# Two hybrid decoder layers on one core: attention by pairs of heads, one load for x and the first weights, rotated queries from SBUF, and three pieces of work put elsewhere in the order

## The chip, the cores and the metric

The kernel runs on 1 core of one Trainium2 chip. The metric is the device time of one execution in microseconds (us). Three runs of the kernel before gave 914.79, 917.12 and 917.61 us, so the median is 917.12 us. A separate profiled execution took 915.54 us; its trace spans 913.8 us from the first to the last instruction.

## The reference, cut to what matters

Two layers, one after the other, on x of 256 tokens by 2048 channels, all in float32. Each layer makes one input projection whose columns feed three mixers (a short convolution, multi-head latent attention, RWKV-7), concatenates their gated results, makes one output projection and normalizes.

```python
for l in range(DEPTH):                       # DEPTH = 2
    u = x @ w_in[l]
    (cb, cc, ch, cg, cq, ckv, kpe, mg, rcols, rg) = _split(u, IN_SIZES)
    y_conv = _short_conv_branch(cb, cc, ch, cg, conv_w[l])
    y_mla = _mla_branch(cq, ckv, kpe, mg, q_norm_g[l], w_uq[l], kv_norm_g[l], w_ukv[l], cos, sin)
    y_rwkv = _rwkv7_branch(rcols, rg, ...)
    mix = jnp.concatenate([y_conv, y_mla, y_rwkv], axis=-1)
    x = _layer_norm(DEEPNORM_ALPHA * x + mix @ w_out[l], ln_g[l], ln_b[l])
```

The attention branch has 8 heads. Queries come from `rms(cq) @ w_uq` (128 plain and 64 rotated channels a head), keys and values from `rms(ckv) @ w_ukv` (128 each), and one rotated key part is shared by all heads. Scores are causal; the result is multiplied by `silu(mg)`.

## The kernel before

**Matrix products.** TensorE reads float32 rounded to a shorter form (`F32R`). For accuracy each operand is split into a rounded part and the remainder, and three products are summed: hi·hi, hi·lo, lo·hi (`mm3`, or two instructions in `in_group` where the moving operand holds hi and lo side by side). The split of a tile is one ScalarE copy and one VectorE subtraction (`split_in`, line 205; `split_w` for weights). All VectorE and ScalarE instructions issued through the wrapper carry line 138 in the profile.

**Stages of a layer.** The input projection runs over column groups of 512 in the order k, a, r, v, cq, cc, ch, cb, cg, rg (`MAIN`), then `mla_kv` (`pkv`), `mla_q` (`pq`), then the groups mg0 and mg1, then the output projection `out_proj` (`po` with `hi_wo`) in four groups of 512 columns. Each weight tile is loaded by SyncE (line 394), split, and used by 24 or 16 matmuls. Products accumulate in two PSUM buffers (`acc`) and must be copied out before the second group after them can start.

**What is interleaved.** The mixers are Python generators. `tick()` advances each of them once per weight tile, so their instructions are issued between the projection's matmuls. A planner then puts every engine's instructions in order by a simulated timeline and by priority (`high_priority(n)` moves work n places ahead: `AHEAD` is 1500, `EVICT` is 4000). The result is a fixed order per engine; on the chip an engine waits at the head of its own order. `after(a, b)` and `gather(m, list)` only tell the planner that one instruction comes behind another; on two engines they make no wait on the chip.

**Buffers.** SBUF tiles come from pools by tag. The tag `s8` has 9 buffers of 8 KB per partition, which hold x (4 of them, until mg1 is done), the RWKV operands (`bk`, `ar`, two `gs`, `bkt`, `uvt`), then `mc` (the convolution's result, split), keys `kn`, values `vs`, queries `qn`, and the split attention results. A tile gets the buffer that comes free next in the order of allocation: before the change that is `mc`, `kn`, `vs`, `qn`. `c4` has 5 buffers, `s4` has 6.

**Start.** `load_x` (line 218) and line 394 issue for each step of `STEPS` one load of x and one of the first weight group k: 1, 1, 2, 2, ... chunks of 128 rows. `warm_up` runs `WARM` = 8 matmuls on zeros (`pzero`) first.

**Attention.** `mla_attend` (line 1054) makes one visit per head: `values(h-3)`, `turn(h-2)` (transposes of the probabilities, `ptr`), `scores(h)` (`sc`, softmax), `split_qk(h+1)`, then `yield`: 11 visits. `mla_q` copies `qn` out of PSUM on ScalarE and rotates `qp` with VectorE straight from PSUM (`rope`: a product with cosT, four quarter products with sinT, a sum).

**End of attention.** `gated` multiplies by the gate and leaves its instruction in `st["mark"]`; `mla_gate` splits the result into `ma0`, `ma1`. `out_proj` gets the mark as `begin` and puts behind it a table load with a reciprocal root (`rstd`) on ScalarE, the loads of the residual `xr` and of the norm rows `gb` (lines 1316 and 1319, issued by ScalarE) and the load of `gr` (issued by GpSimd).

**Norm.** `add` adds a finished block to the residual, takes its statistics and multiplies it by the norm weight. `root(1)` makes the last half's statistics into `rstd` and `cw`. `keep_warm` runs `KEEP` = 10 matmuls (`pz`) while that chain is on VectorE.

Of the kernel before, what the change touches and what calls it, by code (L numbers as in the profile page):

```python
# [31 lines left out]
WARM = 8  # L32
# [53 lines left out]
def lay_out(inp):  # L86
# [5 lines left out]
    o["xT"] = inp["x"][0].T.reshape(NKC, P, S).transpose(1, 0, 2)  # L92
# [19 lines left out]
def hybrid_layers(ctx: ExitStack, tc: tile.TileContext, x, positions, xT, w_in, w_out, w_uq, w_ukv, par, wa_in, gb_in,  # L112
# [123 lines left out]
    def warm_up():  # L236

        z = s8("zero", (P, 512))
        V.memset(z, 0.0)
        zr = s8("zeror", (P, 512), F32R)  # L240
        V.tensor_copy(zr, z)
        pz = pm.tile([P, 512], F32, tag="m", name="pzero")
        for i in range(WARM):
            T.matmul(pz, zr[:, 0:P], zr, start=True, stop=True)
# [17 lines left out]
    def rope_tables():  # L262
        ang = sm.tile([P, S], F32, tag="rt", name="ang")
        nn = sm.tile([P, S], F32, tag="rt", name="nn")
        V.tensor_copy(ang, posi)
# [3 lines left out]
        V.tensor_scalar(nn, nn, magic, None, ALU.subtract)  # L269
        c1 = 6.28125  # L270
# [5 lines left out]
        V.tensor_scalar(ang, ang, lim, -lim, ALU.min, ALU.max)  # L276
        A.activation(sinT, ang, AF.Sin, scale=cs[:, K_SG:K_SG + 1])
# [98 lines left out]
    def load():  # L376
# [4 lines left out]
        raw = to = behind = None  # L381
# [10 lines left out]
        if raw is None:  # L392
            raw = wr.tile(shape, F32, tag="raw", name=f"w_{name}_{k0}")
# [346 lines left out]
    def rwkv_pairs(l, st):  # L740
# [29 lines left out]
        for c2 in range(2):  # L770
# [12 lines left out]
            yield  # L783
# [184 lines left out]
    def rope(dst, ps, name):  # L968

        tmp = sm.tile([P, S], F32, tag="rt", name=f"rt_{name}")  # L970
        V.tensor_tensor(dst, ps, cosT, ALU.mult)
        for q in range(4):
            o = slice(q * 32, q * 32 + 32)
            i = slice((q ^ 1) * 32, (q ^ 1) * 32 + 32)
            V.tensor_tensor(tmp[o, :], ps[i, :], sinT[o, :], ALU.mult)
        V.tensor_tensor(dst, dst, tmp, ALU.add)

    def mla_kv(l, st):
# [3 lines left out]
        vs = s8(f"vs{l}", (P, 2, HEADS, P), F32R)  # L982
        for h2 in range(4):
# [21 lines left out]
    def mla_q(l, st):  # L1005
# [3 lines left out]
        for g in range(4):  # L1009
# [40 lines left out]
    def split_keys(st, h):  # L1050
        t = st["qk"][h % 2]
        split_in(t[:, 0, P:384], t[:, 1, P:384], st["kn"][:, h, :])

    def mla_attend(l, st):
# [4 lines left out]
        def split_queries(h):  # L1059
            t = qk[h % 2]  # L1060
            split_in(t[:, 0, 0:P], t[:, 1, 0:P], qn[:, h, P:S])

        def split_qk(h):

            split_queries(h)
            split_keys(st, h)

        gates.clear()
        with tc.high_priority(AHEAD):
            for par in range(2):  # L1070
# [3 lines left out]
                V.tensor_tensor(of(o), qp[r, :, P:S], of(r).bitcast(F32), ALU.subtract)  # L1074
                split_queries(par)
# [3 lines left out]
        def scores(h):  # L1079
            ps = pm.tile([P, 384], F32, tag="m", name=f"sc{l}_{h}")  # L1080
            for q0, k1, o in ((0, 128, slice(0, 128)), (128, 256, slice(128, 384))):
                if q0 == 0:
                    T.matmul(ps[:, o], qn[:, h, 0:P], kn[:, h, 0:k1], start=True, stop=False)
# [17 lines left out]
            for i, o in both:  # L1101
                V.tensor_scalar(s[:, o], s[:, o], mx[:, 4 + i:5 + i], None, ALU.mult)
            live[h] = s

        def turn(h):
            s = live[h]
            pt = pm.tile([P, 3, P], F32, tag="m", name=f"ptr{l}_{h}")
            for i in range(3):
                T.transpose(pt[:, i, :], s[:, i * P:i * P + P], ident)
# [6 lines left out]
        def values(h):  # L1116
            hi, lo, p2 = live.pop(h)
            po = pm.tile([P, S], F32, tag="m", name=f"po{l}_{h}")
            T.matmul(po[:, P:S], vt[:, h, :], p2, start=True, stop=False, skip_group_check=True)
            for i, (v, p) in enumerate(((0, hi), (1, hi), (0, lo))):  # L1120
                T.matmul(po, vs[:, v, h, :], p, start=False, stop=i == 2, skip_group_check=True)
            A.copy(qn[:, h, :], po)

        for h in range(HEADS + 3):
            if h >= 3:
# [314 lines left out]
```

## Time and profile before

| What | before |
|---|---|
| runs, median | 917.12 us (914.79 to 917.61) |
| profiled execution, own time | 915.54 us |
| its span, first to last instruction | 913.8 us |
| TensorE matmul busy | 891.9 us, 98% |
| TensorE weight load busy | 784.9 us, 86% |
| VectorE busy | 689.0 us, 75% |
| ScalarE busy | 485.6 us, 53% |
| GpSimd busy | 23.0 us, 3% |
| loads from HBM | 158.61 MB, 179 GB/s with the writes |

The time minus the span is 1.74 us. PE is TensorE's matmuls, PEld its weight loads, DVE is VectorE, ACT ScalarE, POOL GpSimd, SP SyncE; "ACTq" and "SPq" are loads being issued. A row of the timeline reads: start, duration, engine, line, operation, tiles out<-in, shapes, count, and in brackets the idle time before it with what ended it. A row of the windows view reads: busy time and instruction count of each engine in that stretch, granted TensorE clock, DMA share, GB/s.

### The profile page before, as it was taken

How to read it: one execution, taken by the hardware profiler on the slowest of the kernel's cores; microseconds unless marked ns; L12 is line 12 of the kernel's file. 1: busy time of each engine (PE TensorE's matmuls, PEld its weight loads, DVE VectorE, ACT ScalarE, POOL GpSimd, SP SyncE). 2: the span in 40 equal slices, each digit the busy share in tenths (PEclk: the TensorE clock that was granted, in tenths of full speed). 3: DMA queues.
4: the chain of work that ended last, by engine and by line, in shares of the span. 5: the costliest groups of instructions: out<-in, count | busy, mean ns of one | idle time of the engine just before them, and what ended most of it. 6: DMA issues, size and time to landing. Idle time of an engine off the chain costs nothing.

```text
span 913.8 us, 15981 instructions
## 1 busy us (share of the span) xinstructions
PE 891.9 (98%) x6311; PEld 784.9 (86%) x6311; DVE 689.0 (75%) x1166; ACT 485.6 (53%) x753; POOL 23.0 (3%) x47
## 2 busy tenths in 40 slices
PE   8999999999999999999999999999999999999996
PEld 7888888888889898788898888888888898987895
DVE  6788979976669977466765889799766699863875
ACT  5677445454447566444246873554444566664430
POOL 1220000000000000000020000000000000000000
PEclk9999999999999999999999999999999999999998
DMA  8865664676444654596476556646754356546932
GB/s 317 251 181 164 206 176 127 193 200 171 142 126 147 185 162 141 169 342 205 160 230 185 141 182 197 172 131 202 191 179 135 105 179 186 159 124 202 338 124 92
DMA packets 67548, 164.97 MB, mean 181 GB/s; under 512 B 15431, under 2 KB 24695, under 8 KB 67463
## 3 DMA queue, kind: packets, MB, share of 16 engines
q1 hardware_dynamic: 59712, 150.36, 54.7%
q10 hardware_dynamic: 5072, 9.57, 3.3%
q0 software_dynamic: 2688, 4.03, 1.5%
q8 instruction: 49, 0.80, 0.4%
q14 instruction: 27, 0.21, 0.1%
HBM read 158.61 MB, written 5.32 MB: 179 GB/s over the span
## 4 chain that ended last, share of the span: by engine, by line
PE 92%; DVE 4%; ACT 1%; issue 1%; DMA 1%; ACTq 0%; SPq 0%; DVEq 0%
PE u_mg L437 6%; PE po L337 6%; PE po L338 6%; PE po L339 6%; PE u_cc L437 3%; PE u_cg L437 3%; PE u_v L437 3%; PE u_cq L437 3%; PE u_mg L439 3%; PE u_ch L437 3%; PE u_cb L437 3%; PE u_r L437 3%; PE u_rg L437 3%; PE u_a L437 3%; PE u_rg L439 2%; PE u_cg L439 2%
## 5 line engine op out<-in xcount | busy, mean ns | idle before, releaser
L138 DVE TENSOR_TENSOR lo_wo<-w_wo,hi_wo 128x1024 fp32r<-128x1024 f32 x57 | 69.2, 1224 | 52.7 <-ACT hi_wo L138 51.9
L138 ACT CAST hi_wo<-w_wo 128x1024 fp32r<-128x1024 f32 x57 | 59.4, 1051 | 66.0 <-PE po L339 43.6
L437 PE MATMUL u_mg<-x,hi_mg 128*128 128x512 f32 x256 | 89.6, 393 | 2.0 <-DVE rt_q L138 2.0
L439 PE MATMUL u_mg<-x,lo_mg 128*128 128x256 f32 x256 | 71.3, 278 | 0.0
L437 PEld LDWEIGHTS u_mg<-x,hi_mg 128*128 128x128 f32 x256 | 48.0, 187 | 12.6 <-ACT qk L138 1.8
L337 PE MATMUL po<-hi_wo,ma 128*128 128x512 f32 (+1 forms) x128 | 46.8, 365 | 2.1 <-ACT ma L138 2.1
L439 PEld LDWEIGHTS u_mg<-x,lo_mg 128*128 128x128 f32 x256 | 48.2, 188 | 0.0
L138 ACT CAST hi_mg<-w_mg 128x1024 fp32r<-128x1024 f32 x32 | 33.6, 1049 | 24.8 <-PE u_mg L437 12.3
L339 PE MATMUL po<-hi_wo,ma 128*128 128x512 f32 (+1 forms) x128 | 46.6, 364 | 0.0
L338 PE MATMUL po<-lo_wo,ma 128*128 128x512 f32 (+1 forms) x128 | 46.5, 363 | 0.0
L437 PE MATMUL u_a<-x,hi_a 128*128 128x512 f32 x128 | 45.5, 398 | 0.9 <-DVE kx L138 0.9
L437 PE MATMUL u_cg<-x,hi_cg 128*128 128x512 f32 x128 | 46.0, 400 | 0.0
L437 PE MATMUL u_cc<-x,hi_cc 128*128 128x512 f32 x128 | 45.8, 400 | 0.0
L437 PE MATMUL u_cq<-x,hi_cq 128*128 128x512 f32 x128 | 45.6, 396 | 0.0
L437 PE MATMUL u_v<-x,hi_v 128*128 128x512 f32 x128 | 45.3, 399 | 0.0
L437 PE MATMUL u_r<-x,hi_r 128*128 128x512 f32 x128 | 45.2, 394 | 0.0
L437 PE MATMUL u_rg<-x,hi_rg 128*128 128x512 f32 x128 | 45.1, 392 | 0.0
L138 DVE TENSOR_TENSOR lo_mg<-w_mg,hi_mg 128x1024 fp32r<-128x1024 f32 x32 | 38.9, 1222 | 8.2 <-ACT hi_mg L138 8.0
L437 PE MATMUL u_cb<-x,hi_cb 128*128 128x512 f32 x128 | 44.5, 394 | 0.0
L437 PE MATMUL u_ch<-x,hi_ch 128*128 128x512 f32 x128 | 44.5, 394 | 0.0
L339 PE MATMUL u_k<-x,lo_k 128*128 128x256 f32 x128 | 37.1, 290 | 1.0 <-DVE lo_k L138 1.0
L337 PE MATMUL u_k<-x,hi_k 128*128 128x256 f32 x128 | 36.9, 288 | 0.9 <-ACT hi_k L138 0.9
(414 smaller groups left out, 2803.4 us busy)
## 6 DMA issues: line engine op xcount, KB each, us to landing
w_wo<-in_w_out_dram SPq DMA_DIRECT2D x64, 512.0 KB, 4.3
w_mg<-in_w_in_dram SPq DMA_DIRECT2D x32, 512.0 KB, 4.4
w_a<-in_w_in_dram SPq DMA_DIRECT2D x16, 512.0 KB, 5.0
w_r<-in_w_in_dram SPq DMA_DIRECT2D x16, 512.0 KB, 3.9
w_v<-in_w_in_dram SPq DMA_DIRECT2D x16, 512.0 KB, 3.9
w_cq<-in_w_in_dram SPq DMA_DIRECT2D x16, 512.0 KB, 3.8
w_cc<-in_w_in_dram SPq DMA_DIRECT2D x16, 512.0 KB, 4.1
w_ch<-in_w_in_dram SPq DMA_DIRECT2D x16, 512.0 KB, 3.6
```

The costliest lines, as they stand in the source:

```text
L138: inst = call(*args, **kwargs)
L337: m = T.matmul(o, lh, rh, start=first, stop=False, skip_group_check=True)
L338: T.matmul(o, lh, rl, start=False, stop=False, skip_group_check=True)
L339: T.matmul(o, ll, rh, start=False, stop=last, skip_group_check=True)
L437: T.matmul(ps[:, b, :].rearrange("p (i t) -> p i t", i=2), hi[:, k, c], x2, start=k0 + k == 0, stop=False, skip_group_check=True)
L439: T.matmul(ps[:, b, 0:S], lo[:, k, c], x2[:, 0, :], start=False, stop=k0 + k == NKC - 1, skip_group_check=True)
```

## The change

1. The host lays x and layer 0's group k side by side, so `load_first` brings both in one load per step, into `s8` tiles. The tiles of zeros go to `c4`. `WARM` is 7.
2. `rope_tables` becomes a generator: it starts a tick after group k and gives way twice.
3. `rope` does the sine products first and the cosine product in place. `mla_q` copies `qp` out of PSUM on ScalarE and rotates it in SBUF, at priority `AHEAD`.
4. The convolution's split `mc` no longer waits for the end of the RWKV chain but for the allocation of `vs`, so the order in `s8` becomes `kn`, `vs`, `mc`, `qn`.
5. `mla_attend` visits two heads at a time (6 visits of two yields); `values` fills one PSUM tile for two heads and copies it out at once; first matmuls are planned behind the splits and softmaxes that they need; `p2` gets a pair-wide tile with two buffers instead of one.
6. `st["mark"]` is the ScalarE copy of the last `ma` split, so the residual, norm rows and table load of `out_proj` come behind it.
7. In `add`, the last block's product with the norm weight moves behind `cw`; `keep_warm` runs 3 narrow and 9 wide matmuls.

```diff
-WARM = 8
+WARM = 7
-    o["xT"] = inp["x"][0].T.reshape(NKC, P, S).transpose(1, 0, 2)
+    o["xT"] = np.concatenate([inp["x"][0].T.reshape(NKC, P, S), w[0, :, :, 0].reshape(NKC, P, 512)], 2).transpose(1, 0, 2)
...
-    def load_x(k0, n):
-        xt = c4(f"xt0_{k0}", (P, n, S))
-        in_turn(1, nc.sync.dma_start(xt, xT[:, k0:k0 + n, :]))
+    def load_first(k0, n):
+        t = s8(f"first{k0}", (P, n, S + 512))
+        in_turn(1, nc.sync.dma_start(t, xT[:, k0:k0 + n, :]))
         with tc.high_priority():
-            for j in range(0, n, 2):
-                m = min(2, n)
-                t, at = xs[(k0 + j) // 4], (k0 + j) % 4
-                split_in(t[:, 0, at:at + m, :], t[:, 1, at:at + m, :], xt[:, j:j + m, :])
+            to, at = xs[k0 // 4], k0 % 4
+            split_in(to[:, 0, at:at + n, :], to[:, 1, at:at + n, :], t[:, :, 0:S])
         if k0 == 14:
-            load_constants(xt[:, 0, :])
+            load_constants(t[:, 0, :])
+        return t[:, :, S:].rearrange("p k (i c) -> p i k c", i=2)
...
-        z = s8("zero", (P, 512))
+        z = c4("zero", (P, 512))
...
     def rope_tables():
+        yield from until("k0")
+        yield
...
         if name == "k0":
-            load_x(k0, nk)
-            raw = s4(f"w_first{k0}", shape) if k0 < 10 else None
+            raw = load_first(k0, nk)
+            ready[name, k0] = k0, split_w(raw, f"{name}_{k0}", None, None)
+            return
...
     def rope(dst, ps, name):
-        V.tensor_tensor(dst, ps, cosT, ALU.mult)
         for q in range(4):
...
+        V.tensor_tensor(dst, ps, cosT, ALU.mult)
         V.tensor_tensor(dst, dst, tmp, ALU.add)
...
         vs = s8(f"vs{l}", (P, 2, HEADS, P), F32R)
+        done.add(f"vs{l}")
...
                 A.copy(qn[:, 2 * g:2 * g + 2, :], pn)
-                rope(qp[:, g, :], pe_, f"q{l}_{g}")
+                A.copy(qp[:, g, :], pe_)
+            with tc.high_priority(AHEAD):
+                rope(qp[:, g, :], qp[:, g, :], f"q{l}_{g}")
...
-            p2 = sm.tile([P, P], F32, tag="p2", name=f"p2{l}_{h}", bufs=1)
+            if h % 2 == 0:
+                st["p2"] = sm.tile([P, 2, P], F32, tag="rs", name=f"p2{l}_{h}", bufs=2)
+            p2 = st["p2"][:, h % 2]
...
+        def values(i):
+            po = pm.tile([P, 2, S], F32, tag="m", name=f"po{l}_{i}")
+            for j in range(2):
+                h = 2 * i + j
+                hi, lo, p2 = live.pop(h)
+                m = T.matmul(po[:, j, P:S], vt[:, h, :], p2, start=j == 0, stop=False, skip_group_check=True)
+                if j == 0:
+                    gather(m, [st["soft"]] if i < HEADS // 2 - 1 else [])
+                for n, (v, p) in enumerate(((0, hi), (1, hi), (0, lo))):
+                    T.matmul(po[:, j, :], vs[:, v, h, :], p, start=False, stop=n == 2, skip_group_check=True)
+            A.copy(qn[:, 2 * i:2 * i + 2, :], po)
+        pairs = HEADS // 2
+        for i in range(pairs + 2):
+            if i >= 2:
+                values(i - 2)
+            for h in (2 * i, 2 * i + 1):
+                if 1 <= i <= pairs:
+                    turn(h - 2)
+            for h in (2 * i, 2 * i + 1):
+                if i < pairs:
+                    scores(h)
+                if h + 2 < HEADS:
+                    split_qk(h + 2)
...
-        st["mark"] = V.scalar_tensor_tensor(y, g, 0.5, y, ALU.mult, ALU.mult)
+        V.scalar_tensor_tensor(y, g, 0.5, y, ALU.mult, ALU.mult)
...
-            split_in(*hl2([m], i * 2), st["qn"][:, half * 4 + i * 2:half * 4 + i * 2 + 2, :])
+            st["mark"] = split_in(*hl2([m], i * 2), st["qn"][:, half * 4 + i * 2:half * 4 + i * 2 + 2, :])[0]
...
-        yield from until(f"chain{l}")
+        yield from until(f"vs{l}")
         m = t["mc"] = pair(f"mc{l}")
...
-            if (h, g) != (1, 0):
+            if (h, g) != (1, 0) and (h, at) != (1, 256):
                 V.tensor_tensor(z, z, gs[g][:, 0, at:at + n], ALU.mult)
...
+            if h:
+                z = zs[3][:, 1, 256:512]
+                after(V.tensor_tensor(z, z, gs[3][:, 0, 256:512], ALU.mult), v)
...
-            for _ in range(KEEP):
-                T.matmul(pz, ms[3][:, 0, 0, 0:P], ms[3][:, 0, 0:2, :], start=True, stop=True)
+            for i in range(KEEP + 2):
+                T.matmul(pz[:, 0:P] if i < 3 else pz, ms[3][:, 0, 0, 0:P],
+                         ms[3][:, 0, 0, 0:P] if i < 3 else ms[3][:, 0, 0:2, :], start=True, stop=True)
...
-                rope_tables()
+                run(rope_tables())
```

More of the change, by code (lines that the diff above doesn't have):

```diff
@@ L236, in warm_up @@
     def warm_up():
-        z = s8("zero", (P, 512))
+        z = c4("zero", (P, 512))
         V.memset(z, 0.0)
-        zr = s8("zeror", (P, 512), F32R)
+        zr = c4("zeror", (P, 512), F32R)
         V.tensor_copy(zr, z)
@@ L269, in rope_tables @@
         V.tensor_scalar(nn, nn, magic, None, ALU.subtract)
+        yield
         c1 = 6.28125
@@ L276, in rope_tables @@
         V.tensor_scalar(ang, ang, lim, -lim, ALU.min, ALU.max)
+        yield
         A.activation(sinT, ang, AF.Sin, scale=cs[:, K_SG:K_SG + 1])
@@ L380, in load @@
             return
-        raw = to = behind = None
+        to = behind = None
         src = src[:, :, k0:k0 + nk, :] if len(src.shape) == 4 else src[:, k0:k0 + nk, :]
@@ L391, in load @@
             to = t[:, 0], t[:, 1]
-        if raw is None:
-            raw = wr.tile(shape, F32, tag="raw", name=f"w_{name}_{k0}")
+        raw = wr.tile(shape, F32, tag="raw", name=f"w_{name}_{k0}")
         i = nc.sync.dma_start(raw, src)
@@ L782, in rwkv_pairs @@
             A.copy(qs[:, c2 * 2:c2 * 2 + 2], pq_)
-            yield
+        yield
         st["qs"] = qs
@@ L1051, in split_keys @@
         t = st["qk"][h % 2]
-        split_in(t[:, 0, P:384], t[:, 1, P:384], st["kn"][:, h, :])
+        st[f"split{h}"] = [split_in(t[:, 0, P:384], t[:, 1, P:384], st["kn"][:, h, :])[1]]
     def mla_attend(l, st):
@@ L1060, in split_queries @@
             t = qk[h % 2]
-            split_in(t[:, 0, 0:P], t[:, 1, 0:P], qn[:, h, P:S])
+            return split_in(t[:, 0, 0:P], t[:, 1, 0:P], qn[:, h, P:S])[1]
         def split_qk(h):
-            split_queries(h)
+            v = split_queries(h)
             split_keys(st, h)
+            st[f"split{h}"].append(v)
         gates.clear()
@@ L1073, in mla_attend @@
                 A.copy(of(r), qp[r, :, P:S])
-                V.tensor_tensor(of(o), qp[r, :, P:S], of(r).bitcast(F32), ALU.subtract)
-                split_queries(par)
+                v = V.tensor_tensor(of(o), qp[r, :, P:S], of(r).bitcast(F32), ALU.subtract)
+                st[f"split{par}"] += [v, split_queries(par)]
+        st["split0"] += st["split1"]
         live = {}
@@ L1082, in scores @@
                 if q0 == 0:
-                    T.matmul(ps[:, o], qn[:, h, 0:P], kn[:, h, 0:k1], start=True, stop=False)
+                    m = T.matmul(ps[:, o], qn[:, h, 0:P], kn[:, h, 0:k1], start=True, stop=False)
+                    gather(m, st[f"split{h}"])
                     T.matmul(ps[:, o], qp[:, h // 2, 0:P], kpe[:, h % 2 * P:h % 2 * P + P], start=False, stop=True)
@@ L1101, in scores @@
             for i, o in both:
-                V.tensor_scalar(s[:, o], s[:, o], mx[:, 4 + i:5 + i], None, ALU.mult)
+                v = V.tensor_scalar(s[:, o], s[:, o], mx[:, 4 + i:5 + i], None, ALU.mult)
             live[h] = s
+            st["soft"] = v
         def turn(h):
@@ L1113, in turn @@
+            p2 = st["p2"][:, h % 2]
             A.copy(p2, pt[:, 2])
             live[h] = hi, lo, p2
[L1116 to L1122, printed above, removed]
@@ L1124, in mla_attend @@
-        for h in range(HEADS + 3):
-            if h >= 3:
-                values(h - 3)
-            if 2 <= h < HEADS + 2:
-                turn(h - 2)
-            if h < HEADS:
-                scores(h)
-            if 2 <= h + 1 < HEADS:
-                split_qk(h + 1)
-            if h == 3:
+        def values(i):
[9 more added lines that the diff above has]
+            A.copy(qn[:, 2 * i:2 * i + 2, :], po)
@@ L1134, in mla_attend @@
+        pairs = HEADS // 2
[10 more added lines that the diff above has]
+                    split_qk(h + 2)
+            if i == 2:
                 done.add(f"heads{l}")
-            if h >= 4 and h % 2 == 0 and f"mg{(h - 4) // 4}{l}" in done:
-                gated(l, st, (h - 4) // 2)
+            if i >= 2 and f"mg{(i - 2) // 2}{l}" in done:
+                gated(l, st, i - 2)
+            yield
```

4 lines of the change are left out of this document (3 added, 1 removed).

## The prediction, made before the changed kernel ran

> **What bounds the kernel now.** I read the page first: the span, the busy line, the chain that ended last.
>
> ```profile
> span 913.8 us, 15981 instructions
> PE 92%; DVE 4%; ACT 1%; issue 1%; DMA 1%; ACTq 0%; SPq 0%; DVEq 0%
> L437 PE MATMUL u_mg<-x,hi_mg 128*128 128x512 f32 x256 | 89.6, 393 | 2.0 <-DVE rt_q L138 2.0
> ```
>
> TensorE sets the end: 92% of the chain is matmuls. The change takes no matmul out but one of eight on zeros at the start, and adds some filler in `keep_warm`. It can only win where TensorE stands still. So the second view is who TensorE waited for, in total, over the whole run (us, times, longest):
>
> ```profile
> PE pkv L337 <- ACT vt L138: 2.9, 2, 1.4
> PE po L337 <- ACT ma L138: 2.1, 2, 1.0
> ...
> PE cwt L1259 <- DVE cw L138: 1.4, 1, 1.4
> PE u_k L339 <- DVE lo_k L138: 1.0, 2, 0.8
> PE xt L1280 <- PE pz L1312: 0.9, 1, 0.9
> PE u_k L337 <- ACT hi_k L138: 0.9, 1, 0.9
> PE u_a L437 <- DVE kx L138: 0.9, 1, 0.9
> PE po L338 <- DVE lo_wo L138: 0.5, 2, 0.3
> ...
> PE pq L337 <- ACT qn L138: 0.4, 1, 0.4
> PE pq L337 <- ACT vt L138: 0.4, 1, 0.4
> ```
>
> With the 2.0 us of `rt_q` in the row above these are 13.4 us. That is nearly all that this change can reach: about 1.5% of the span, in ten places, each with another cause. The busy shares of VectorE and ScalarE say little here; in each place it is one late instruction that matters. I go through the places in the order of the change's parts.
>
> **Start: one load for x and w, seven matmuls on zeros.** The chain, then four windows, then two rows of single instructions:
>
> ```profile
> 3.78 5.88 DMA w_first<-in_w_in_dram
> 9.69 1.05 ACT hi_k L138
> ...
> 12.04 0.38 PE u_k L339
> ```
>
> ```profile
> 0.00:4.00 4.00, 1.97 (x5) 1.60 (x6) 1.46 (x4) 1.69 (x2) 1.45 (x6) 1.00 0.38 121
> 4.00:8.00 4.00, 4.00 (x19) 3.63 (x17) 1.32 (x3) 1.84 (x4) 0.00 (x0) 1.00 0.86 258
> 8.00:12.00 4.00, 2.19 (x15) 1.57 (x13) 2.28 (x4) 2.19 (x4) 0.00 (x0) 1.00 1.01 364
> 16.00:20.00 4.00, 4.00 (x36) 4.00 (x35) 3.61 (x5) 3.07 (x5) 0.00 (x0) 1.00 1.05 388
> ```
>
> ```profile
> 10.64 0.61 ACT L138 CAST x<-xt 128x512 fp32r<-128x512 f32 x1
> L244 PE MATMUL pzero<-zeror 128*128 128x512 f32 x8 | 3.8, 652 | 2.0 <-DVE zeror L138 2.0
> ```
>
> Steady matmuls begin at 12.04, when the weights of the third step are split; they landed at 9.69, and that load was the sixth to be issued, at 3.78. In the new kernel it is in the third load. The first three loads hold 4 x 128 rows x 768 numbers x 4 bytes = 1.57 MB. The old kernel had moved 0.48 MB by 4.0 (121 GB/s); the other 1.09 MB take 3.0 us at the 364 GB/s of the third window and 4.2 at the 258 of the second. So they land at 7.0 to 8.2, that is 1.5 to 2.7 earlier. Off that goes the cast of x (0.61), which arrives with the weights now and is ahead of them on ScalarE: 0.9 to 2.1. I take 1.6. If the merged load lands no sooner, x's cast makes it 0.6 worse; the bounds are -0.6 and 2.1. After these a step is 0.79 MB, 2.2 us at 364 GB/s, and its 24 matmuls take 2.7 (36 in 4.00 us, the fourth window), so an early start isn't lost again there. The matmul on zeros that goes is 3.8/8 = 0.47 us ahead of the first `u_k`; it is inside the 1.6, since the wait at 12.04 decides. The new tiles share `s8`: five are free, and later loads wait for a split, not the first three.
>
> At 652 ns a matmul on zeros is slower than the 393 of `u_mg` of the same shape. The Trainium skill (TensorE: Matmul & The Clock Gate, Part 1) says that the array starts at half rate and that a time of activity, not a count of matmuls, ends this. By that rule the `u_k` matmuls that move forward by 0.47 us run at half rate, and an estimate of the start's gain would be 1.4 in place of 1.6 us.
>
> **Tables of the rotation as a generator.** `u_a` waits 0.9 us for the last `kx`, which frees the accumulator. ScalarE is at this then:
>
> ```profile
> 39.63 1.28 ACT L138 ACT_TABLE_LOAD   x1
> ```
>
> That is the load for the sines, between the third and the fourth `kx`. Planned a few ticks later, it comes behind `kx`. I take 0.7 of 0 to 0.9. What is late next is the rotated key, which nothing on TensorE needs before attention.
>
> **Values' buffer.** ScalarE's and TensorE's timelines, layer 0:
>
> ```profile
> 266.64 0.57 ACT L138 COPY kn<-pkv 128x512 f32<-128x512 f32 x1
> 271.48 0.65 ACT L138 CAST vs<-pkv 128x256 fp32r<-128x256 f32 x2
> ```
>
> ```profile
> 271.24 0.69 PE L808 MATMUL py<-st,ar 64*64 64x64 f32 x32
> 273.37 0.39 PE L337 MATMUL pkv<-hkv,hi_ukv 128*128 128x256 f32 x1 [1.43 <-ACT vt L138]
> ```
>
> Keys leave PSUM at 266.64, values of the same group only at 271.48, when the RWKV chain's last products are running: `vs` holds the buffer that comes free last. The third `pkv` group then waits 1.43 us for the accumulator. In the new order `vs` takes the place in the line that `kn` had, `kn` that of `mc`, both free by 266.64, and `mc` is left with the late one. Then the copies come at once and the 2.9 us of both layers go, perhaps the 0.4 of `pq` behind it too. I take 2.9 of 1.4 to 3.3. `mc` costs this:
>
> ```profile
> L337 PE MATMUL po<-hi_wo,mc x16: 387/389/398, 354.9 to 381.3; 128*128 128x512 f32 x16
> L138 DVE TENSOR_TENSOR mc<-cy,mc x2: 687/690/692, 245.9 to 246.5; 128x512 fp32r<-128x512 f32 x2
> ```
>
> Its split is needed at 354.9 and has 80 us; but two times 0.69 us of VectorE per layer move from 246 to after 272, into the stretch that is full (next part). Price 0 to 2.8; I take 1.0.
>
> **Rotation from SBUF.** TensorE in layer 1, then VectorE, ScalarE and the window in layer 0:
>
> ```profile
> 752.49 0.47 PE L437 MATMUL u_mg<-x,hi_mg 128*128 128x512 f32 x1 [1.62 <-DVE rt_q L138]
> ```
>
> ```profile
> 298.95 1.72 DVE L138 TENSOR_TENSOR rt_q<-pq,sinT 32x256 f32<-32x256 f32 x4
> 295.19 0.58 ACT L138 COPY qn<-pq 128x512 f32<-128x512 f32 x1
> 296.00:300.00 4.00, 4.00 (x34) 4.00 (x35) 3.93 (x7) 1.83 (x4) 0.00 (x0) 1.00 0.50 140
> ```
>
> The accumulator is held by VectorE's rotation, and VectorE is busy 3.93 of 4.00 us. ScalarE, busy 1.83, takes the copy: half of the 128x512 that cost 0.58 us, so between 0.29 and 0.58. VectorE's own work doesn't shrink; its five products only leave the accumulator's way. Of 2.0 us I take 1.6 (0 to 2.0): one of the copies may stand behind a weight cast, as `qn` did for the 0.4 of the waits, and for that and the eight copies I put a cost of 0.4 (0 to 1.6).
>
> **End of attention, and heads by two.** ScalarE, TensorE, then VectorE's first use of the residual, layer 1:
>
> ```profile
> 835.54 1.28 ACT L138 ACT_TABLE_LOAD   x1
> 836.95 0.60 ACT L138 CAST ma<-qn 128x512 fp32r<-128x512 f32 x1
> ```
>
> ```profile
> 826.35 0.38 PE L1119 MATMUL po<-p,vt 128*128 128x128 f32 x2
> 833.43 0.38 PE L1119 MATMUL po<-p,vt 128*128 128x128 f32 x2
> 837.60 0.50 PE L337 MATMUL po<-hi_wo,ma 128*128 128x512 f32 x1 [1.04 <-ACT ma L138]
> ```
>
> ```profile
> 847.33 1.28 DVE L138 SCALAR_TENSOR_TENSOR xr<-xr,po 128x512 f32<-128x512 f32 x2
> ```
>
> The last split of the attention result stands on ScalarE behind `out_proj`'s table load (1.28) and load issues. The new mark puts all of these behind it: more than the 1.04 us that TensorE waits, in both layers. The residual and norm rows are issued some 2 us later; they are first used at 847.33, about 10 us after the split, which hides that; without this cover it would cost those 2 us. Attention's matmuls stay the same in number, and the planned order adds no instruction. Its last two visits stand 7.1 us apart, at places where the planner expects inputs, not where the inputs are. Three visits of one head drain the pipeline before, two of a pair after, so I expect the end no later. Of 2.1 + 0.5 us I take 2.1 (0 to 2.6). New is that the second head's scores reuse the PSUM tile that the pair's result has just left: ScalarE's copy may hold up TensorE. I put 0.4 (0 to 3.2, eight visits by 0.4, the size of the smallest waits above).
>
> **Norm.** VectorE at the end:
>
> ```profile
> 903.88 0.43 DVE L138 TENSOR_TENSOR xr<-xr,gb 128x256 f32<-128x256 f32 x1
> ```
>
> This product leaves the chain to `cw`: 0.43 a layer. Layer 0's wait of 0.9 before `xt` can lose that; in layer 1 the product comes back ahead of the next VectorE step. I take 0.4 of 0 to 0.9. The filler's two extra matmuls lie in that wait; without it they cost under 0.8 (two of the 393 ns above).
>
> **Sum.** 1.6 + 0.7 + 2.9 + 1.6 + 2.1 + 0.4 = 9.3 us gained, 1.0 + 0.4 + 0.4 = 1.8 lost: 7.5 less. The profiled execution took 915.54 us (its span and 1.74), so the same execution would take 908.0. It lies 1.6 below the median of the runs, 917.12; I put the new median half of that above its own execution: 908.8. With every term at its good end (11.8 off, no costs) it is 904.5; the bad ends together (0.8 gained, 7.6 lost) are a loss of 6.8.
>
> **Rivals.** First, VectorE stays full behind the values: with `mc`'s splits and the same rotation there, 296 to 312 only changes what is late, and `u_mg` now waits for its weights' split. Then the terms of rotation and half of the values go: 7.5 - 1.6 - 1.4 = 4.5 off, 911.8 with the same step to the median. For it speaks 3.93 of 4.00; against it that weights' splits are planned with priority.
>
> Second, every wait comes back elsewhere, because the planner makes a new order of 15981 instructions from times that aren't the chip's: the start gains nothing, and new waits of 0.4 to 1.4 like those listed, some eight of them, eat the rest. Result 916, no change that can be told. Against it: the values and the mark are removed causes, not guesses of the planner.
>
> Third, slower: attention's tail. `values` of a pair is planned behind the softmax of the next pair. If the last pair's `values` come one step of 7.1 us later than 833.43, the wait at 837.60 grows by 7.1 in each layer. The other terms give 7.5 - 2.1 = 5.4; 14.2 - 5.4 = 8.8 more, 925. From 2.7 us of lateness per layer on it outweighs the rest. For it: both layers end attention close to the need (833.43 and 836.56). Against it: fewer visits drain.
>
> **How the numbers follow.** Forecast 0.50, its own range 905 to 912; VectorE full 0.22; waits come back 0.16; slower 0.12. A measurement of this kernel can tell about 0.3%, 2.75 us, so faster is below 914.4: nearly all of the forecast and most of the first rival, 0.70. Same 0.18, slower 0.12. The range from 903.5 to 917 holds all but the slower rival and a few hundredths on either side.
>
> **What would show it.** Right: steady `u_k` from about 10.4; `vs` copied within 1 us of `kn`, no wait at the third `pkv`; `u_mg` not waiting for `rt_q`; `ma` cast ahead of the table load, no wait at `po`; matmul busy time the same within 1 us. Wrong: `u_k` later than 11.5, a wait of over 1 us at `sc` or `po`, or attention's last `po` more than 3 us nearer to the output projection's need.

## The result, and the profile after

The new kernel takes 908.12 us, the median of four runs (906.56 to 909.28); the kernel before, run beside it, 916.04 (914.79 to 917.61). The ratio is 0.991, with a 95% interval from 0.989 to 0.994. The prediction was 908.8. The profiled execution of the new kernel took 909.28 us, its span is 907.5.

The page of the new kernel: span, busy line, chain.

```profile
span 907.5 us, 16003 instructions
...
PE 893.1 (98%) x6314; PEld 786.7 (87%) x6314; DVE 687.5 (76%) x1166; ACT 486.1 (54%) x752; POOL 24.6 (3%) x47
...
PE 95%; DVE 2%; ACT 1%; DMA 1%; issue 0%; DVEq 0%; SPq 0%; ACTq 0%
```

The matmuls' share of the chain went from 92 to 95%. Whom TensorE waited for, all over the span (us in total, times, longest):

```profile
PE u_a L441 <- DVE u_a L138: 3.1, 1, 3.1
PE pzero L244 <- DVE zeror L138: 1.9, 1, 1.9
PE cwt L1286 <- DVE cw L138: 1.0, 1, 1.0
PE u_k L343 <- DVE lo_k L138: 0.8, 1, 0.8
PE lw L1295 <- DVE ct L138: 0.6, 1, 0.6
PE po L341 <- DVE xr L138: 0.5, 1, 0.5
PE pq L341 <- ACT vt L138: 0.5, 2, 0.2
PE xt L1307 <- PE pz L1339: 0.4, 1, 0.4
```

The waits of before at `pkv` (2.9), at `po` on `ma` (2.1) and at `u_mg` on `rt_q` (2.0) are gone. One has grown: `u_a` waited 0.9 for `kx` and now waits 3.1. The windows around it, new kernel first, then the kernel before (busy time and count of PE, PEld, DVE, ACT, POOL, then the granted clock, DMA share, GB/s):

```profile
40.00:44.00 4.00, 1.41 (x8) 0.94 (x7) 3.42 (x7) 3.40 (x7) 0.00 (x0) 0.96 0.82 227
44.00:48.00 4.00, 3.51 (x11) 3.03 (x12) 1.10 (x4) 3.92 (x8) 2.79 (x6) 0.50 0.63 142
48.00:52.00 4.00, 4.00 (x18) 3.39 (x17) 2.35 (x2) 1.43 (x2) 2.25 (x4) 0.68 0.64 136
```

```profile
44.00:48.00 4.00, 3.61 (x20) 3.15 (x21) 2.84 (x6) 3.94 (x7) 3.28 (x7) 1.00 0.81 159
48.00:52.00 4.00, 4.00 (x24) 3.45 (x23) 2.85 (x3) 1.97 (x3) 2.31 (x3) 1.00 0.96 257
```

After the wait the clock is at half rate: 11 and 18 matmuls fit where 20 and 24 did. PE's busy time, 3.51 and 4.00, does not show this; the count and the clock do.

To see where the rest went I took the time from each matmul's start to the next one's start and added it up by the tile it writes. The sum over all tiles is the span, a wait counts with the matmul ahead of it, and a slower rhythm shows too. New kernel minus kernel before, us, both layers (groups that differ by less than 0.25 left out):

| tiles | difference | what lies there |
|---|---|---|
| `pzero`, `u_k` | -2.1 | start |
| `u_a` | +4.9 | layer 0: the wait and the half rate |
| `pg`, `u_cq` | -1.3 | layer 0, RWKV products |
| `u_ch`, `u_cb` | +1.7 | no wait in them |
| `py`, `pkv` | -2.8 | waits of `pkv` on `vt` |
| `pq`, `sc` | -3.1 | waits on the rotation and on `qn` (2.4 of it) |
| `u_mg` | +0.7 | no wait in them |
| `po` | -3.9 | waits on `ma`, attention's products |
| `pz`, `cwt` | -0.3 | norm |
| sum | -6.2 | the spans differ by 6.3 |

So three things were to be settled: why `u_a` lost 4.9, where `pg` won and `u_ch`, `u_cb`, `u_mg` lost without a wait, and which part earned what.

### The profile page after: what moved, and what is told of

It reads as the page before. It is cut to its first block, busy times and chain, and to the rows that moved or that the text cites. A ratio compares the mean times of both kernels' runs of the same rounds, so it can differ in the third digit from the quotient of the medians.

```text
span 907.5 us, 16003 instructions
## 1 busy us (share of the span) xinstructions
PE 893.1 (98%) x6314; PEld 786.7 (87%) x6314; DVE 687.5 (76%) x1166; ACT 486.1 (54%) x752; POOL 24.6 (3%) x47
## 4 chain that ended last, share of the span: by engine, by line
PE 95%; DVE 2%; ACT 1%; DMA 1%; issue 0%; DVEq 0%; SPq 0%; ACTq 0%
PE po L341 7%; PE u_mg L441 7%; PE po L343 7%; PE po L342 6%; PE u_a L441 4%; PE u_cc L441 3%; PE u_cg L441 3%; PE u_mg L443 3%; PE u_v L441 3%; PE u_cb L441 3%; PE u_ch L441 3%; PE u_cq L441 3%; PE u_rg L441 3%; PE u_r L441 3%; PE u_rg L443 2%; PE u_cg L443 2%
## 5 line engine op out<-in xcount | busy, mean ns | idle before, releaser
L441 PE MATMUL u_a<-x,hi_a 128*128 128x512 f32 x128 | 48.1, 415 | 3.1 <-DVE u_a L138 3.1
L138 DVE TENSOR_TENSOR lo_rg<-w_rg,hi_rg 128x1024 fp32r<-128x1024 f32 x16 | 19.6, 1223 | 23.2 <-ACT hi_rg L138 23.2
```

The source lines that it names most:

```text
L138: inst = call(*args, **kwargs)
L441: T.matmul(ps[:, b, :].rearrange("p (i t) -> p i t", i=2), hi[:, k, c], x2, start=k0 + k == 0, stop=False, skip_group_check=True)
```

## Experiments

Each was timed beside the kernel before on the same chip. Ratios are to the kernel before.

### Constants asked for earlier

ScalarE's timelines differ in one place. In the kernel before the first `kx` (`u_k` mixed with its shifted self, which needs the constants) follows the fourth cast of `hi_a`, in the new one the fifth. There are four buffers for `hi_a`, so later casts wait until `u_a`'s matmuls have used the earlier ones, and everything behind such a cast waits too. ScalarE, the kernel before (fourth cast, first `kx`):

```profile
32.14 1.05 ACT L138 CAST hi_a<-w_a 128x1024 fp32r<-128x1024 f32 x1 [1.83 <-PE u_k L338]
33.10 0.47 ACT L138 ACTIVATE kx<-u_k,pc 128x256 f32<-128x256 f32 x1
```

and the new kernel (fifth cast, first `kx`; then what stands around the last `kx`):

```profile
32.85 1.05 ACT L138 CAST hi_a<-w_a 128x1024 fp32r<-128x1024 f32 x1 [1.55 <-PE u_a L441]
33.80 0.47 ACT L138 ACTIVATE kx<-u_k,pc 128x256 f32<-128x256 f32 x1
...
41.33 1.04 ACT L138 CAST hi_a<-w_a 128x1024 fp32r<-128x1024 f32 x1 [0.55 <-PE u_a L441]
42.28 0.58 ACT L138 COPY u_a<-u_a 128x512 f32<-128x512 f32 x1
42.76 0.48 ACT L138 ACTIVATE kx<-u_k,pc 128x256 f32<-128x256 f32 x1
```

TensorE, the new kernel, then the kernel before:

```profile
41.13 0.28 PE L443 MATMUL u_a<-x,lo_a 128*128 128x256 f32 x1
44.49 0.79 PE L441 MATMUL u_a<-x,hi_a 128*128 128x512 f32 x1 [3.08 <-DVE u_a L138]
```

```profile
44.39 0.51 PE L437 MATMUL u_a<-x,hi_a 128*128 128x512 f32 x1 [0.85 <-DVE kx L138]
```

The last `kx` frees the accumulators of `u_k`. Before, it ran at 42.90, beside matmuls. Now it is planned behind the first half of `u_a`, so the second half is given the first half's own accumulator and waits until that has been copied out (42.28, then VectorE's sum at 43.75). The second half starts no earlier than before, 44.49 against 44.39: what the start had won up to there is spent in this wait, and the half rate comes on top. The edit asks for the constants earlier:

```diff
-        if k0 == 14:
+        if k0 == 8:
             load_constants(t[:, 0, :])
```

> The new kernel with one number changed: the parameter block, the rotation's constants and the positions are asked for after the sixth step of x instead of after the last. Theory A (the 3.08 us wait of u_a at 44.49, and the half-rate stretch behind it, come from ScalarE's written order: the first kx stands behind the fifth cast of hi_a, the order is set from when the plan expects the constants, and by asking for them earlier the kx move ahead by one cast or two): u_a waits at most 0.9 us between its two halves, the granted clock stays at 1.00 from 44 to 52 us, and the time is 4 to 6 us below the new kernel, 902 to 905. Theory B (VectorE or the lateness of the constants themselves, or the merged loads' traffic, makes the wait): the wait stays near 3, the time within 1.5 of 908. Theory C (earlier constants push the weights back in the queue): the wait goes but steady u_k stand still for 0.5 to 1.5 us somewhere between 10 and 30 us, and the time is 904 to 907.

Measured: 904.86 us (904.02 to 905.82), ratio 0.987 (0.985 to 0.988). The wait at `u_a` is gone, and so is the half rate:

```profile
44.00:48.00 4.00, 4.00 (x23) 3.45 (x22) 4.00 (x4) 3.13 (x5) 0.00 (x0) 1.00 0.75 179
48.00:52.00 4.00, 4.00 (x25) 3.50 (x24) 3.57 (x7) 3.33 (x4) 0.00 (x0) 1.00 0.77 239
```

On ScalarE the first `kx` now runs at 31.13, ahead of the fourth cast. `u_a` costs 6.0 us less than in the new kernel. Theory A holds. Theory B does not fit: the edit makes the constants land earlier too, but in the new kernel the parameter block that `kx` needs, asked for at 19.6, had landed by about 25, over 8 us before the first `kx`. Its order on ScalarE was the cause.

### The wait filled with matmuls

```diff
             ps = acc(f"u_{name}{l}_{i}")
+            if (l, name, i) == (0, "a", 1):
+                pf = pm.tile([P, 512], F32, tag="m", name="pfill")
+                for _ in range(12):
+                    f = T.matmul(pf, xs[0][:, 0, 0, 0:P], xs[0][:, 0, 0:2, :], start=True, stop=True)
+                    after(f, m_)
...
-                        T.matmul(ps[:, b, 0:S], lo[:, k, c], x2[:, 0, :], start=False, stop=k0 + k == NKC - 1,
+                        m_ = T.matmul(ps[:, b, 0:S], lo[:, k, c], x2[:, 0, :], start=False, stop=k0 + k == NKC - 1,
```

`m_` is the last matmul of the first half.

> The new kernel with twelve extra matmuls of 128x512 (results not used) between the two halves of u_a, where TensorE stood still for 3.08 us and then ran at half rate for about 6 us. The wait's cause stays. Theory A (the half rate follows from the idle): the clock stays at 1.00 from 44 to 52 us, the first half-tile of u_a after it starts at about the same time as before (44.5, at most 0.5 later), and the kernel gains the 2.7 us that the half rate cost, 905 to 906. Theory B (the half rate comes from something else at this place, such as the power of the other engines): the clock still falls to 0.5, and the time is that of the new kernel or up to 0.5 more.

Measured: 908.64 us (907.84 to 909.03), ratio 0.991 (0.989 to 0.992): no gain, though theory A's mechanism is there.

```profile
42.11 2.89 PE L438 MATMUL pfill<-x 128*128 128x512 f32 x12
45.36 0.50 PE L446 MATMUL u_a<-x,hi_a 128*128 128x512 f32 x1 [0.35 <-DVE u_a L138]
```

```profile
44.00:48.00 4.00, 3.65 (x20) 2.82 (x19) 1.98 (x6) 3.94 (x9) 1.92 (x4) 1.00 0.67 192
```

The clock stays at 1.00, so the half rate follows from the stand-still. `u_r` begins at 57.60 instead of 59.39, although this execution's start was some 0.9 later, so about 2.7 us were won. But `u_cc` begins at 135.64 instead of 136.04: by then only 0.4 is left. In between lie the `pg` matmuls. The chain in the new kernel, then in this one (start, us):

```profile
112.22 2.53 PE pg L654 x32
121.54 1.99 PE pg L654 x32
```

```profile
110.31 2.53 PE pg L659 x32
117.08 1.08 PE pg L659 x8
119.75 1.98 PE pg L659 x24
```

The planner has put the second 32 in two pieces, as in the kernel before. Eight by themselves start 112 ns apart; in the long pieces most of the matmuls start in twos, 4 to 14 ns apart, one on each half of the array's rows. The eight use the halves in turn too; why they don't pair is not shown. With what the cut does to the neighbours it costs 1.3 us. (The Trainium skill, TensorE: Matmul & The Clock Gate, Part 3, says that matmuls on different rows overlap with starts about 4 ns apart; these traces agree.)

### The merged load alone, and the tables made at once

In the kernel before, the first part of the change with its layout on the host, and nothing else:

```diff
-WARM = 8
+WARM = 7
...
-            load_x(k0, nk)
-            raw = s4(f"w_first{k0}", shape) if k0 < 10 else None
+            raw = load_first(k0, nk)
+            ready[name, k0] = k0, split_w(raw, f"{name}_{k0}", None, None)
+            return
```

> The kernel before with the first part of the change alone: x and the first weights in one load, seven matmuls on zeros, zeros in another buffer. Theory A (the merged load brings the start forward by 2 us and, by moving the plan's times, also puts the first kx one cast later on ScalarE, so that the u_a wait and the half rate come with it): steady u_k from about 9.9, the u_a wait is about 3 instead of 0.85, the clock falls to 0.5 behind it, and the net is a loss: 2.1 gained, 4.9 lost, 2.5 to 3 us slower than before. Theory B (the wait comes from the generator of the tables): steady u_k from 9.9, u_a wait 0.85 or less, 2 us faster than before.

Measured: 916.38 us, ratio 0.999 (0.998 to 1.000): no difference that can be told. The wait came with it, and the clock fell; the waits, then the window:

```profile
PE u_a L437 <- DVE u_a L138: 3.1, 1, 3.1
```

```profile
44.00:48.00 4.00, 2.19 (x7) 1.90 (x8) 2.43 (x6) 3.97 (x9) 1.47 (x3) 0.68 0.71 221
```

Theory A holds in kind: the merged load causes the wait. The loss of 2.5 to 3 us that it foretold did not come. By tiles `u_a` lost 3.5, `pg` and `u_cq` won 1.3 (here too `pg` is in two whole pieces), the start won 0.7 in this execution, `pq` and `pkv` won 1.4, and `sc` lost 1.2 because the wait on `rt_q` grew from 2.0 to 3.2. The gain at `pg` was in neither theory.

The other suspect, in the new kernel:

```diff
-        yield from until("k0")
-        yield
...
-                run(rope_tables())
+                for _ in rope_tables():
+                    pass
```

> The new kernel with the rotation's tables made at once, as before, instead of in four parts as a generator. Theory A (the merged load's effect on the order is the cause): the u_a wait stays at 2.5 to 3.5 us with the half rate behind it, 906 to 910. Theory B (the tables as a generator push VectorE's part of u_a back): the wait falls to 0.9 or less, and the time to 903 to 905.

Measured: 909.85 us (one run); the wait stays, with the half rate behind it.

```profile
PE u_a L439 <- DVE u_a L138: 3.1, 1, 3.1
```

So the generator neither causes nor cures it.

### The other parts, each alone in the kernel before

The values' buffer:

```diff
         vs = s8(f"vs{l}", (P, 2, HEADS, P), F32R)
+        done.add(f"vs{l}")
...
-        yield from until(f"chain{l}")
+        yield from until(f"vs{l}")
```

> The kernel before with one part of the change: vs is announced as soon as its buffer is made, and mc's split waits for that instead of for the chain's end. Theory A (the third pkv of each layer waits for the copy of vt into the buffer only because the chain and mc's split held it): the two waits of 1.43 us at pkv fall to 0.3 or less, the split of mc finds room on VectorE, and the kernel is 2.5 to 2.9 us faster. Theory B (mc's split, now in the stretch where VectorE is full, makes kn or rt_q late): the pkv waits go, but the wait for rt_q grows from 2.0 to 3 or more, and the gain is 0 to 1.5.

Measured: 917.87 us, ratio 1.001 (1.000 to 1.002). The waits at `pkv` are gone, but:

```profile
PE u_mg L437 <- DVE rt_q L138: 4.5, 2, 2.3
```

Theory B: `mc`'s splits in the full stretch of VectorE push the rotation back, and `u_mg` pays. By tiles 3.0 won at `py` and 0.4 at `pq`, 4.8 lost at `sc`, `u_mg` and `pkv`. The gain of 0 to 1.5 that theory B left did not come.

The rotation from SBUF, with the new order of products in `rope`:

```diff
-                rope(qp[:, g, :], pe_, f"q{l}_{g}")
+                A.copy(qp[:, g, :], pe_)
+            with tc.high_priority(AHEAD):
+                rope(qp[:, g, :], qp[:, g, :], f"q{l}_{g}")
```

> The kernel before with one part of the change: ScalarE copies the queries' rotated part out of PSUM and VectorE rotates the copy in SBUF. Theory A (u_mg waits for the rotation only because it holds the PSUM buffer): the wait on rt_q, 2.0 us in two places, and the 0.4 of pq on qn fall to 0.3 together, 1.6 to 2.4 us faster. Theory B (the copies push qn back on ScalarE, and pq waits for them): the rt_q wait goes, pq waits 1 to 1.5 for qn or qp, and the gain is under 1.

Measured: 913.56 us, ratio 0.997 (0.996 to 0.999), 2.6 us. No wait on `rt_q` is left, and none on `qn`. Theory A. (Its profiled execution, 918.11, is the longest of its ten runs: at the start `u_k` waited 2.1 us for a cast of its weights, and the clock was at half rate from 11.99 to 18.82 behind that. So the medians are read here.)

The mark, with its old place in `gated` dropped:

```diff
-            split_in(*hl2([m], i * 2), st["qn"][:, half * 4 + i * 2:half * 4 + i * 2 + 2, :])
+            st["mark"] = split_in(*hl2([m], i * 2), st["qn"][:, half * 4 + i * 2:half * 4 + i * 2 + 2, :])[0]
```

> The kernel before with one part of the change: what the output's loads of weights are ordered behind is the split of ma on ScalarE instead of the last gate on VectorE. Theory A (the two waits of po on the cast of ma, 1.04 us each, come from the order on ScalarE that this mark sets): the po waits fall to 0.3 or less in total on ma, 1.8 to 2.1 us faster. Theory B (it is the longer attention by single heads that makes ma late, and the pairs that end it earlier): the two waits stay within 0.3 of 2.1 us, and the time within 0.5 of before.

Measured: 912.94 us, ratio 0.996 (0.995 to 0.998), 3.3 us. The waits on `ma` are gone. Theory A; its 1.8 to 2.1 lies at the low end of what the interval allows. The wait on `rt_q` fell to 0.8 too, for which no theory had a reason.

The pairs of heads, all of the change in `mla_attend` and `split_keys`, with the mark still set in `gated`:

```diff
-        for h in range(HEADS + 3):
-            if h >= 3:
-                values(h - 3)
...
+        for i in range(pairs + 2):
+            if i >= 2:
+                values(i - 2)
```

> The kernel before with the attention alone by two heads a visit, the mark where it was. Theory A (the pairs cost nothing and bring nothing by themselves): the waits on ma stay at 2.1, no wait over 0.5 at sc, ptr or po, time within 1.0 of before. Theory B (they end the attention's VectorE work earlier and so take the waits on ma away): po waits on ma at most 0.5, 1.5 to 2.5 faster. Theory C (the last pair adds a step to the chain of softmax, transposes and values): po at the attention's end waits 2 us or more, 3 to 8 slower.

Measured: 918.13 us, ratio 1.002 (1.001 to 1.003). The waits on `ma` are gone here too, which speaks for theory B, but as with the values others took their place:

```profile
PE u_mg L437 <- DVE rt_q L138: 3.0, 2, 2.7
PE pkv L337 <- ACT vt L138: 2.9, 2, 1.4
PE pzero L244 <- DVE zeror L138: 2.0, 1, 2.0
PE pq L337 <- DVE rt_q L138: 2.0, 1, 2.0
```

No theory had this. Each of the mark and the pairs removes the waits on `ma` by itself; values and pairs each make the rotation late, as the merged load does. By the ratios the four alone make 2.6 + 3.3 gained and 1.0 + 1.4 lost, 3.5 us (the 1.0 can't be told from nothing); how they hang together is the next question.

### Parts undone in the faster version

Both in the version with the constants asked for earlier (904.86). First the rotation straight from PSUM again:

```diff
-                A.copy(qp[:, g, :], pe_)
-            with tc.high_priority(AHEAD):
-                rope(qp[:, g, :], qp[:, g, :], f"q{l}_{g}")
+                rope(qp[:, g, :], pe_, f"q{l}_{g}")
```

> The same fastest kernel with the queries rotated straight from PSUM again. Alone in the kernel before, the values' part let the wait on rt_q grow from 2.0 to 4.5 us, and the pairs let it grow to 5.0. Theory A (the rotation from SBUF is what makes room for both, so in the whole it is worth much more than alone): waits on rt_q of 5 to 8 us, 5 to 8 slower than that kernel, 910 to 913. Theory B (it is worth what it brought alone): waits on rt_q of 2 to 3.2, 2 to 3 slower, 907 to 908.

Measured: 916.02 us, ratio 0.999 (0.998 to 1.000), 11 slower than that version. Who TensorE waits for, and layer 0's first matmul of `u_mg` with the windows around it:

```profile
PE u_mg L441 <- DVE rt_q L138: 7.1, 2, 3.6
```

```profile
296.27 0.77 PE L441 MATMUL u_mg<-x,hi_mg 128*128 128x512 f32 x1 [3.56 <-DVE rt_q L138]
```

```profile
292.00:296.00 4.00, 0.71 (x6) 0.51 (x5) 3.92 (x8) 1.93 (x3) 0.00 (x0) 0.86 0.31 64
296.00:300.00 4.00, 3.73 (x11) 3.22 (x12) 3.89 (x7) 0.00 (x0) 0.00 (x0) 0.50 0.58 195
```

Theory A, and more: behind each of the two waits the clock falls to half, which costs another 2.4 us at `u_mg` in each layer. VectorE is busy 3.92 of 4.00; a sum of the RWKV result and a split of weights of `mg` stand ahead of the rotation that TensorE needs. A part that brings 2.6 alone carries 11 in the whole.

Then the attention by single heads again, the mark in `mla_gate` kept:

```diff
-        for i in range(pairs + 2):
-            if i >= 2:
-                values(i - 2)
...
+        for h in range(HEADS + 3):
+            if h >= 3:
+                values(h - 3)
```

> The fastest kernel so far (new kernel, constants asked for after the sixth step of x: 904.86) with the attention by single heads again; everything else of the change stays, the mark at the split of ma too. Theory A (pairs and mark each take the same waits on ma away, so the pairs bring nothing beside the mark): waits on ma stay under 0.3, the time within 1.0 of that kernel. Theory B (the pairs also bring what the mark leaves, the two 0.27 at lo_wo and the place of VectorE's last gates): 0.5 to 1.5 slower. Theory C (the pairs crowd VectorE in the middle, and even with the rotation from SBUF this costs): 1 to 3 faster than that kernel.

Measured: 905.46 us, ratio 0.988 (0.986 to 0.989); the difference to 0.987 is inside the intervals. The trace is 1.8 us longer, all of it at `po`, 0.9 in each layer, of which 0.27 is the wait on `lo_wo`. Theory B by the trace; by the times the pairs' worth can't be told from nothing.

### The slower rhythm

`u_ch` and `u_cb` did not wait, yet each took 22.6 us a layer instead of 22.2. Two small parts were in no run alone: the norm's later product, and one visit less in the making of `qs`, which is in the change but not in its list and diff above. Both in the kernel before:

```diff
-            yield
+        yield
         st["qs"] = qs
...
-            if (h, g) != (1, 0):
+            if (h, g) != (1, 0) and (h, at) != (1, 256):
...
+            if h:
+                z = zs[3][:, 1, 256:512]
+                after(V.tensor_tensor(z, z, gs[3][:, 0, 256:512], ALU.mult), v)
...
-            for _ in range(KEEP):
+            for i in range(KEEP + 2):
```

> The kernel before with the two small parts that no run so far had alone: one visit less in the making of qs ahead of the chain of states, and the norm's later product with its changed filler. Theory A: the wait at xt falls from 0.9 to 0.4 and that at cwt from 1.4 to 1.0, that at lw grows by 0.2 to 0.3, 0.5 to 1.0 faster by these; and the 256 matmuls of u_ch and u_cb of each layer, which took 22.19 us each before and 22.61 after without any wait, take 22.61 here, as the visit changes the order around them, so that the net is within 1 of the kernel before. Theory B (that slower rhythm comes only with other parts together): u_ch and u_cb stay at 22.19 and the kernel is 0.5 to 1.0 faster.

Measured: 917.26 us, ratio 1.000 (0.999 to 1.002). Theory A: `u_ch` and `u_cb` take 22.6 here, and the waits at the norm are 0.4 (`xt`), 1.0 (`cwt`) and 0.6 (`lw`) as foretold. Then the visit put back in the version with the earlier constants:

```diff
             A.copy(qs[:, c2 * 2:c2 * 2 + 2], pq_)
-        yield
+            yield
         st["qs"] = qs
```

> The fastest kernel so far (904.86) with the visit of the making of qs put back: its two halves are made in two visits, as in the kernel before. Theory A (the one visit less put u_ch and u_cb into the slower rhythm): u_ch and u_cb take 22.2 us in each layer instead of 22.6, no wait grows, 1.7 faster by these four groups, 903 or a little less. Theory B (the slower rhythm came with the norm's part): they stay at 22.6, and the time is within 1 of 904.9. Theory C (without the visit less the chain of states ends later, and values or pkv wait again): a wait of 0.5 to 1.5 at pkv or py in each layer, 1 to 3 slower.

Measured: 902.64 us (901.61 to 902.92), ratio 0.984 (0.982 to 0.987), the fastest of all; its span is 901.1. `u_ch` (duration in ns, least/median/most) in the new kernel, then here:

```profile
L441 PE MATMUL u_ch<-x,hi_ch x128: 395/398/404, 163.9 to 634.0; 128*128 128x512 f32 x128
L443 PE MATMUL u_ch<-x,lo_ch x128: 277/281/284, 164.2 to 634.2; 128*128 128x256 f32 x128
```

```profile
L441 PE MATMUL u_ch<-x,hi_ch x128: 392/394/395, 159.1 to 628.0; 128*128 128x512 f32 x128
L443 PE MATMUL u_ch<-x,lo_ch x128: 274/277/280, 159.3 to 628.2; 128*128 128x256 f32 x128
```

Theory A: all 1.7 us of these groups come back and no wait grows. The span is 1.1 shorter than with the earlier constants alone (902.2), since small differences elsewhere take part of it back; by the ratios it is 2.1 us, with intervals that just overlap. That this visit picks the rhythm of `u_ch` and `u_cb` is shown. What makes the two rhythms isn't.

## Why the prediction was right, point by point

The time was right to 0.7 us, and the likeliest case came in. That it is so close is luck. The tables' place was off by 5.6 us (0.7 less was forecast, 4.9 more came), and values, rotation and attention together brought 9.8 us where their terms, less their costs, make 4.8. These two errors, each far larger than the miss, nearly cancelled. The signs named for being right came (at `po` the 0.5 for the residual stayed, as before), but for one: matmul busy time grew by 1.2, where within 1 was said.

**Rope tables: predicted -0.7, and the step that failed.** The place got 4.9 us slower. The prediction put the small `kx` wait before `u_a` down to ScalarE's table load for the sines. That load did move behind the last `kx` (43.65 behind 42.76), also where the tables are made at once, and it brought nothing, since the last `kx` ran hardly earlier (42.90 before). The runs show another cause: the start's own change moves the plan's times, ScalarE's `kx` go one weight cast later, and the second half of `u_a` then waits for the first half's accumulator. The prediction priced the earlier start only by what TensorE gains there and never asked which instruction would be planned later for it. And it priced waits at their length: this one of 3.1 costs another 2.7 through the clock, as the filled wait shows.

**Start: predicted -1.6.** "From about 10.4" was said for steady `u_k`; it comes at 9.93 instead of 12.04. The chain, TensorE's row and the window of the new kernel:

```profile
1.67 5.35 DMA first<-in_xT_dram
```

```profile
9.93 0.39 PE L343 MATMUL u_k<-x,lo_k 128*128 128x256 f32 x1 [0.76 <-DVE lo_k L138]
```

```profile
4.00:8.00 4.00, 4.00 (x22) 3.07 (x21) 2.38 (x5) 2.80 (x6) 0.00 (x0) 1.00 1.03 428
```

In this pair of profiles the gain is 2.1, but starts scatter: the last matmul of `u_k` begins at a median of 31.7 in six profiles with the old loads and of 30.85 in eight with the new. About 0.8 is what holds. The first `u_k` did run slower, as the estimate of 1.4 supposed: in the kernel before they start 0.21 us apart until the clock changes at 7.42, and 0.12 apart behind it; in the new one it changes at 6.17. But 0.2 us is lost in the scatter. The third load landed at 7.02, the early end of the 7.0 to 8.2 worked out, since the loads of 768 KB move 428 GB/s where 364 had been the better of the two rates used. With the `u_a` wait the merged load by itself gains nothing. So the second rival was right about the start, but with one new wait of 3.1 and not some eight small ones.

**Values' buffer: predicted -2.9 and +1.0 for `mc`.** The 2.8 came. The price of `mc`'s splits was named rightly as the rotation's lateness and undersized for the kernel alone (2.5 more wait at `rt_q`, and 4.8 by tiles with the slower stretches behind it, where 1.0 stood and 2.8 was the bound); in the whole no wait of it is left, since the rotation no longer holds PSUM.

**Rotation from SBUF: predicted -1.6, cost 0.4.** 3.1 in the sum by tiles; a copy costs ScalarE 0.38 and delays nothing. The first rival, "VectorE stays full", saw the right pressure: VectorE is just as full there in the new kernel (3.97 of 4.00 from 296 to 300). But the wait that it foretold, of `u_mg` for its weights' split, is in no row; where the rotation holds PSUM again, the wait is for the rotation, and that is what the part removed. The term took the part as it stands alone (2.6 measured); among the other parts it is worth 11.

**End of attention: predicted -2.1, cost 0.4.** 3.9 came. All of the waits on `ma` and `lo_wo` are gone (2.6), and the attention's own products take 0.65 less in each layer. The waits on `ma` were credited to the mark, and the mark alone is enough for them; so are the pairs. The feared PSUM coupling shows in no row. The slower rival, attention's tail, did not come: there is no wait at `sc` or `ptr`, and none at `po` but the 0.5 for the residual that was there before.

**Norm: predicted -0.4.** 0.3: `xt` 0.9 to 0.4, `cwt` 1.4 to 1.0, and `lw` up by 0.2 in the waits.

**Not in the sum at all:** `pg` in whole pieces, 1.3 won; the slower rhythm of `u_ch` and `u_cb`, 1.7 lost, brought by the visit left out, and 0.7 lost at `u_mg`, also without a wait but not by this visit: with it put back `u_mg` still takes 44.86 us a layer instead of 44.50. The prediction counted on matmuls keeping their time where nothing waits, and took their busy time as the sign (within 1 us). The page has 893.1 after 891.9, but busy time is the wrong sign: a new order changes how matmuls sit beside each other, and that is worth as much as a wait.

## What to carry to other kernels

Where an order is planned, a part that starts something earlier can move other instructions later, and it is worth nothing if the next release does not come earlier too: before costing the gain, look for in-order neighbours on the copying engine, above all a constant's first user behind a cast that waits for a buffer. Judge parts together: take one away from the whole (11 us here) as well as adding it alone (2.6), since the part that frees an accumulator pays for those that load the engine holding it. And when a trace's waits don't add up to the change in span, add up start-to-start times by tile; busy time hides half rate and slower rhythms.

## What the runs showed of the hardware that was not expected

**Half rate after a short stand-still.** Past the start's zeros and ahead of the last norm, no wait of 1.4 to 2.0 us lowered the clock; one of 2.1 did (rotation alone, before 11.63). Of two waits of 2.25 us in the same kernel (values' buffer alone), one did and one didn't. They ended at 300.18 in layer 0 and at 752.90 in layer 1; windows from 1.8 and 1.1 us behind that:

```profile
302.00:306.00 4.00, 4.00 (x16) 3.39 (x16) 3.86 (x10) 1.05 (x1) 0.00 (x0) 0.62 0.78 242
...
754.00:758.00 4.00, 4.00 (x25) 3.49 (x24) 3.90 (x10) 1.05 (x1) 0.00 (x0) 1.00 0.68 201
```

Waits of 2.65, 3.1 (in three kernels) and 3.6 (twice) all did, and the half rate lasted from 3 to 6 us beyond the restart. What came on top of the wait was 1.0 (values alone: 46.07 us for `u_mg` in layer 0, 45.09 in layer 1) to 2.7 us (the new kernel).

The traces also hold the times at which the clock changes, and these account for the difference, though no run was made to test it. In all fourteen traces the changes lie whole steps of 3.413 us apart: in the new kernel 43.72, 50.54 and 903.87, which is 2 and then 250 steps. The half rate behind the waits named here lasted one step (3.4 us: merged load alone, values alone) or two (6.8: all others). By them, what counts is how much of a wait lies in one step. Of the 2.25 us that lowered the clock 2.0 lay in one step; of the 2.25 that didn't, 1.5 and 0.75 in two. In the steps before the falls behind these waits TensorE stood still for 1.9 to 2.7 us; other steps before the last norm had 1.6 at most. One fall does not fit: at 459.14 in the run of the rotation alone the step before had 1.0; why the clock fell there is open. The Trainium skill (TensorE: Matmul & The Clock Gate, Part 1) tells of half rate after an idle window of about 3.4 us that runs freely; the steps agree with such a window, but here it did not have to be idle throughout.

**Two rhythms at full clock.** The same pair of matmuls runs at 346.7 ns or at 353.3 ns (22.19 or 22.61 us by 64 pairs), with a granted clock of 1.00, no wait, and the same operands; a change of order ahead of them, one visit less in the making of `qs`, switches whole groups. The cause is open.
